# First layer's expert gate and up with the weights as stationary operand, half of the second layer's modulation on VectorE, final sums as columns

## The chip, the cores and the metric

The kernel runs on one core of one Trainium2 chip. The metric is the device time of one execution in microseconds; the median of three runs before the change is 1820.4 us (1817.2 to 1823.0).

## What is computed

Two layers over 512 latent and 256 context tokens of width 1024, all in fp32. Each layer mixes tokens (an mLSTM, a convolution and a Fourier group between one input and one output projection) and then routes tokens to 16 experts. The part that matters here, cut:

```python
def expert_choice_ffn(xn, w_router, w_gate, w_up, w_down):
    cap = EC_CAPACITY_FACTOR * n // N_EXPERTS
    aff = jax.nn.softmax(jnp.einsum('bnd,de->bne', xn, w_router).astype(jnp.float32), axis=-1)
    gate, idx = lax.top_k(jnp.swapaxes(aff, 1, 2), cap)
    xs = xn[bidx, idx]
    hid = jax.nn.silu(jnp.einsum('becd,edf->becf', xs, w_gate)) * jnp.einsum('becd,edf->becf', xs, w_up)
    ys = jnp.einsum('becf,efd->becd', hid, w_down) * gate[..., None].astype(xn.dtype)
    return jnp.zeros_like(xn).at[bidx, idx].add(ys)
...
    for l in range(DEPTH):
        mod = silu_c @ w_ada[l] + b_ada[l]
        sh1, sc1, gt1, sh2, sc2, gt2 = jnp.split(mod[:, None, :], N_ADA, axis=-1)
...
    return _rms(x, g_final).astype(x.dtype)
```

In the first layer latent and context tokens are both routed, each in its own set (64 and 32 tokens an expert); in the second only latent tokens are.

## The kernel before, in words

The program writes TensorE's order by hand; the order on the other engines is left to the framework's scheduler. Activations stand with features on the partitions. Each layer has three parts: the mixer (input projection `product`, L492, with a three-term split of the weights made by ScalarE L424 and VectorE L427), the output projection (eight blocks, the same `product`), and the expert stage. Small work that is not urgent hangs in `fills`: generators that `product` advances by a credit, so that their instructions land between its own.

One of these is `ada1`: the modulation vectors of the second layer, three rounds of `ada_round` (L284 to L297). A round streams 16 blocks of `w_ada` past two vectors on TensorE (L286, 32 x 256 in four column groups), copies the sums (L292) and turns them with four small products (L295). Its loads go over GpSimd's queue into a ring of 19 buffers. What is left of it is drained in the routing, before the gathered tokens are turned.

The expert stage works on pairs of experts, in the order gate of pair p+1, down of p, up of p+1. Weights come as 1 MB tiles (two blocks of 128 rows of an expert's matrix), eight tiles for a projection of a pair, loaded on SyncE's queue into `wreg` as buffers come free. `wide` runs one projection in four quarters. The tokens are the stationary operand, 32 of them in each column group of the array, and the weights run by in rows of 512: L1451 for the latent tokens (two experts x 64), L1461 for the context tokens (two experts x 32, in two halves). `gate` takes the Silu on ScalarE (L1487, L1489), `up` multiplies on VectorE (L1495, L1497). The hidden rows then have tokens on the partitions, so `up` queues transposes (L1503, 12 a pair) and copies (L1504) that `down` needs. Ahead of that the tokens of a pair are gathered by GpSimd (L1371), transposed on TensorE in `turn` (L1397, 8 for a latent pair, 8 for two context pairs) and modulated (L1402, L1404). `down` leaves its rows on the partitions of their tokens, and GpSimd adds them to a buffer in memory (L1555). In the second layer the tokens come from a one-hot product (L1394) and the last `down` is split in four with the final norm behind it: squares on ScalarE (L1693), summed by `rows` on TensorE (L1701), copied (L358) and turned into columns (L361).

Of the kernel before, what the change touches and what calls it, by code (L numbers as in the profile page):

```python
# [14 lines left out]
D = 1024  # L15
# [34 lines left out]
ADA1_RATE, AREG, ADA_XTK = 0.3, 19, 1.2  # L50
NACC = 6
VLAG = 0.0, 2.5
# [105 lines left out]
def build(nc, tc, xT, ctxT, params, w_ada, w_gates, w_in, w_out, w_router, w_e_gate, w_e_up, w_e_down,  # L158
          dft_l, dft_c, dft_ch, outT):
    RA_N, RB_N = 12288, 4608  # L160
    TOTAL = 53000 - RA_N - RB_N
# [3 lines left out]
    def body(A, RB, PS, scr, xrow, acc):  # L165
# [166 lines left out]
        def ada_scale(l, dst, m, gcol):  # L332
            for v in range(2):
                dve.scalar_tensor_tensor(dst[:, v], MOD[l][:, v, m * 8:(m + 1) * 8], 1.0, pc(l, gcol, 8),
                                         op0=OP.add, op1=OP.mult)
# [63 lines left out]
        for l in range(2):  # L399
# [712 lines left out]
            if not last:  # L1112
                areg = [mem.alloc(1024) for _ in range(AREG)]

                def ada1():
                    ring = Ring(areg)
                    for r in range(3):
                        yield from ada_round(1, r, ring, 5, pool, some=ADS[1])
                    ada_scale(1, A1[1], 1, P_G1)
                    ada_scale(1, A2[1], 4, P_G2)  # L1120
# [4 lines left out]
                fills.append(ada1f)  # L1125

# [12 lines left out]
            def load_experts(firsts=(), most=1000):  # L1139
                while len(wtiles) < min(wtaken[0] + len(wreg), len(wq), most):  # L1140
# [30 lines left out]
            for db in range(KB):  # L1171
# [22 lines left out]
                if db == 4:  # L1194
                    ride(0)
                for s in outs:
# [4 lines left out]
            ride(1)  # L1201
            fills.clear()
# [102 lines left out]
            if not last:  # L1305
                ada1f.drain()
                mem.free(areg)
# [30 lines left out]
            if not last:  # L1338
                slc_r, SLC = new(512)
                htc_r, hTc = new(4, 128)  # L1340
# [17 lines left out]
            XSp, XSq = {}, {}  # L1358
            if not last:
                xg_r = [mem.alloc(D) for _ in range(3)]  # L1360
                xs_r = [mem.alloc(KB * 128) for _ in range(2)]
                xgr = Ring(xg_r)
                xc_r = [mem.alloc(KB * 128) for _ in range(2)]
            fetched, gathers = {}, []

            def fetch_rows(s, i):

                t = fetched[s, i] = V((0, D, wp[4 + (s == CTX)][2]) if i == 0 else xgr.next(), D)
# [17 lines left out]
            def turn(s, i, hf):  # L1386
                def f():
                    dst = (XSp if s == LAT else XSq)[i]
                    b = bank67().rearrange("p (j t) -> p j t", j=4)
                    for j in range(4):  # L1390
                        db = 4 * hf + j
                        if last:
                            for c in range(4):
                                pe.matmul(b[:, j], XT[2 + c][:, db * 128:db * 128 + 128], onehots[i][:, c],  # L1394
                                          start=c == 0, stop=c == 3)
                        else:
                            pe.transpose(b[:, j], fetched[s, i][:, db * 128:db * 128 + 128], ident)  # L1397
# [473 lines left out]
```

## Time and profile before

| what | us |
|---|---|
| median of three runs | 1820.4 |
| the profiled execution | 1825.71 |
| its span | 1823.9 |
| TensorE busy | 1715.1 (94%) |
| weight loads of TensorE busy | 944.6 (52%) |
| VectorE busy | 628.5 (34%) |
| ScalarE busy | 447.5 (25%) |
| GpSimd busy | 150.7 (8%) |

Over the whole span TensorE is busy, but the page's slices show what stands behind that. In forty slices of 45.6 us, TensorE has nine tenths or more in nearly all; the DMA engines have nine tenths from slice 11 to 21 (the first layer's expert stage, about 400 GB/s) and again from slice 31 to 39 (the second layer's, 420 GB/s). The chain that ended last is followed back only to the second layer; in it DMA has 18% of the span and TensorE 14%. Matmuls are pipelined, so the time between the starts of equal instructions tells what one costs, and the idle time in brackets tells whether the engine waited.

### The profile page before, as it was taken

The page shows a single profiled execution, that of the slowest core. Times are in us where ns is not written, and L with a number is a line of the kernel's source. Part 1 is how long each engine was busy: PE and PEld are TensorE (multiplying, and loading weights), DVE is VectorE, ACT ScalarE, POOL GpSimd, SP SyncE. Part 2 cuts the span into 40 slices and gives each one's busy share as a digit, 9 for nine tenths or more (in the row PEclk, how much of TensorE's full clock was granted, in tenths as well). Part 3 has the DMA queues.
Part 4 walks back from the last instruction along what each step waited for, and adds up shares of the span by engine and source line. Part 5 has one row for each costly group of instructions (what it writes and reads, how often), then busy time and mean ns, then how long its engine had stood idle before and what let it go on. Part 6 is the DMA issues. An engine that isn't in the chain of part 4 may idle for free. (4 is left out here: it accounts for less than half of the span.)

```text
span 1823.9 us, 27692 instructions
## 1 busy us (share of the span) xinstructions
PE 1715.1 (94%) x11728; PEld 944.6 (52%) x11728; DVE 628.5 (34%) x1384; ACT 447.5 (25%) x861; POOL 150.7 (8%) x193
## 2 busy tenths in 40 slices
PE   6999999998999999999999999889979999999996
PEld 3678887876333333333233467777744444344433
DVE  4623897424101001001014677865230221112203
ACT  4433354413101101011000552356220101010002
POOL 1111121110101101100100001120000000000000
PEclk8999999998999999999999999999989999999999
DMA  9466344756999999999995113142669999999994
GB/s 384 150 209 195 106 128 157 243 209 233 386 420 402 402 421 403 402 418 404 399 393 213 35 47 97 60 130 96 244 251 421 421 421 420 420 421 421 420 421 193
DMA packets 94525, 529.59 MB, mean 290 GB/s; under 512 B 10177, under 2 KB 13249, under 8 KB 45505
## 3 DMA queue, kind: packets, MB, share of 16 engines
q1 hardware_dynamic: 75776, 459.66, 62.5%
q0 software_dynamic: 18624, 68.17, 11.6%
q8 instruction: 92, 1.51, 0.3%
q14 instruction: 33, 0.26, 0.0%
HBM read 513.10 MB, written 14.68 MB: 289 GB/s over the span
## 5 line engine op out<-in xcount | busy, mean ns | idle before, releaser
L492 PE MATMUL PS<-RA,RB 128*128 128x512 f32 (+1 forms) x2352 | 512.9, 365 | 18.8 <-DVE RB L427 6.0
L1451 PE MATMUL PS<-A 128*32 128x512 f32 (+1 forms) x2256 | 426.7, 595 | 5.8 <-DMA A<-w_e_up 5.2
L492 PEld LDWEIGHTS PS<-RA,RB 128*128 128x128 f32 x2352 | 375.7, 193 | 92.3 <-issue 18.1
L1451 PE MATMUL PS<-WP,A 128*32 128x512 f32 (+1 forms) x2160 | 370.1, 597 | 4.6 <-DMA WP<-w_e_up 4.6
L1451 PEld LDWEIGHTS PS<-A 128*32 128x32 f32 (+1 forms) x2256 | 128.4, 122 | 239.4 <-issue 220.9
L1451 PEld LDWEIGHTS PS<-WP,A 128*32 128x32 f32 (+1 forms) x2160 | 107.8, 117 | 199.0 <-issue 187.1
L1461 PE MATMUL PS<-WP,A 128*32 128x512 f32 x816 | 112.3, 594 | 0.0
L1021 DVE SCALAR_TENSOR_TENSOR A<-A 128x783 f32<-128x783 f32 (+1 forms) x120 | 107.5, 923 | 0.2
L1402 ACT ACTIVATE A<-PS,A 128x128 f32<-128x128 f32 x80 | 36.1, 458 | 245.2 <-DVE A L1404 244.6
L1461 PE MATMUL PS<-A 128*32 128x512 f32 x656 | 95.0, 606 | 0.0
L1504 ACT ACTIVATE A<-PS 128x512 f32<-128x512 f32 x40 | 22.3, 595 | 293.8 <-PE PS L1503 293.8
L424 ACT ACTIVATE RB<-A 128x1024 fp32r<-128x1024 f32 x60 | 63.4, 1059 | 123.7 <-PE PS L492 88.4
L1550 DVE TENSOR_SCALAR A<-PS,A 128x512 f32<-128x512 f32 x6 | 4.5, 751 | 243.9 <-PE PS L1451 243.9
L1517 DVE SCALAR_TENSOR_TENSOR A<-PS,A 128x512 f32<-128x512 f32 x80 | 56.5, 746 | 88.2 <-PE PS L1516 87.5
L1524 DVE SCALAR_TENSOR_TENSOR RB<-PS,A,RB 128x512 fp32r<-128x512 f32 x18 | 13.5, 751 | 205.8 <-ACT RB L1523 205.0
L1404 DVE TENSOR_SCALAR A<-PS,A 128x128 f32<-128x128 f32 x80 | 32.7, 409 | 141.2 <-PE PS L1397 86.0
L427 DVE TENSOR_TENSOR RB<-A,RB 128x1024 fp32r<-128x1024 f32 x50 | 63.0, 1265 | 17.2 <-ACT RB L424 14.7
L1394 PEld LDWEIGHTS PS<-A 128*128 128x128 f32 x512 | 59.3, 196 | 7.2 <-DVE A L1495 4.9
L284 POOL DMA_DIRECT2D A<-w_ada x80 | 42.5, 535 | 235.7 <-PE PS L286 136.3
L1394 PE MATMUL PS<-A 128*128 128x128 f32 x512 | 61.0, 281 | 0.4 <-DVE A L1381 0.4
L1495 DVE TENSOR_TENSOR A<-PS,A 128x512 f32<-128x512 f32 x32 | 22.1, 692 | 109.3 <-PE PS L1451 109.3
L1461 PEld LDWEIGHTS PS<-WP,A 128*32 128x32 f32 x816 | 27.9, 110 | 54.6 <-issue 54.6
(332 smaller groups left out, 1600.9 us busy)
## 6 DMA issues: line engine op xcount, KB each, us to landing
A<-w_e_gate SPq DMA_DIRECT2D x75, 1024.0 KB, 15.7
A<-w_e_up SPq DMA_DIRECT2D x66, 1024.0 KB, 15.3
WP<-w_e_down SPq DMA_DIRECT2D x63, 1024.0 KB, 17.3
A<-w_e_down SPq DMA_DIRECT2D x63, 1024.0 KB, 17.3
WP<-w_e_up SPq DMA_DIRECT2D x62, 1024.0 KB, 14.4
WP<-w_e_gate SPq DMA_DIRECT2D x53, 1024.0 KB, 17.1
A<-w_ada POOLq DMA_DIRECT2D x80, 512.0 KB, 4.7
A<-w_in SPq DMA_DIRECT2D x44, 512.0 KB, 3.6
```

Source lines behind the costliest of these rows:

```text
L284: after(eng.dma_start(w, src[r, hf, k]), firsts if hf == 0 and k < len(ring.regs) else ())
L424: whi.append(act.activation(h, raw[i], AF.Copy))
L427: wlo.append(eng.tensor_tensor(lo, raw[i], h.bitcast(F32), OP.subtract))
L492: pe.matmul(banks[s][:, :LEN[s]], w[:, k], xin[:, j, k, OFF[s]:OFF[s] + LEN[s]], start=k == k0 and i == 0, stop=k == k1 and i == 2)
L1021: dve.scalar_tensor_tensor(o, i, wcol, o, op0=OP.mult, op1=OP.add)
L1394: pe.matmul(b[:, j], XT[2 + c][:, db * 128:db * 128 + 128], onehots[i][:, c], start=c == 0, stop=c == 3)
L1402: act.activation(dst[:, db], b[:, j], AF.Identity, bias=sh_, scale=sc_)
L1404: dve.tensor_scalar(dst[:, db], b[:, j], sc_, sh_, op0=OP.mult, op1=OP.add)
L1451: pe.matmul(B(o + hf)[c:c + wd, :], lhs(k, e)[:, c % 64:c % 64 + wd], w[e][:, a, hf * 512:hf * 512 + 512], start=k == 0, stop=k == KB - 1, ...
L1461: pe.matmul(B(o + 2)[32 * g:32 * g + 32, :], lhsc(k, e), w[e][:, a, hf * 512:hf * 512 + 512], start=k == 0, stop=k == KB - 1, tile_positio ...
L1504: act.activation(dst, b, AF.Copy)
L1517: dve.scalar_tensor_tensor(X[LAT][:, db], b, MOD[l][:, LAT, 40 + db:41 + db], X[LAT][:, db], op0=OP.mult, op1=OP.add)
```

## The change

In the first layer `tall` takes the place of `wide` for gate and up. A weight tile is now laid out as all eight blocks of rows by 256 columns of an expert (`layout`), so that two tiles, one of each expert, make a quarter. A 128 x 128 block of weights is the stationary operand, and the 96 tokens of the expert (64 latent, 32 context, side by side in `XSp`) run by. The result has features on the partitions, as `down` wants it: transposes and copies of hidden rows go, and Silu and product are done a quarter at a time. The context half of `turn` becomes a product of the gathered rows with 64 columns of the identity, for one pair at a time. `down` of the first layer stays as it was.

Of the second layer's modulation only round 0 stays on TensorE. Rounds 1 and 2 are multiplied and added on VectorE (`ada1_rest`, 32 passes over 1024 elements, for the latent vector alone), and `ada1_sums` adds over the partitions with products by ones and turns the sums. Both run as fills of the output projection and end before the routing. The ring has 15 buffers, six for round 0 and nine for the rest.

In the second layer there is one more weight buffer, and the final sums of squares come as columns at once (`cols`). The scratch for GpSimd's descriptors is halved to make room.

```diff
-ADA1_RATE, AREG, ADA_XTK = 0.3, 19, 1.2
+ADA1_RATE, AREG, ADA_XTK = 0.3, 15, 1.2
 NACC = 6
+ADA1V_RATE = 0.55
...
-    TOTAL = 53000 - RA_N - RB_N
+    TOTAL = 55040 - RA_N - RB_N
...
                 def ada1():
-                    ring = Ring(areg)
-                    for r in range(3):
-                        yield from ada_round(1, r, ring, 5, pool, some=ADS[1])
+                    yield from ada_round(1, 0, Ring(areg[:6]), 5, pool, some=ADS[1])
                     ada_scale(1, A1[1], 1, P_G1)
-                    ada_scale(1, A2[1], 4, P_G2)
+                acc_r, ACC = new(2, 2, 1024)
+                def ada1_rest():
+                    ring = Ring(areg[6:])
+                    for r in (1, 2):
+                        for hf in range(2):
+                            for k in range(KB):
+                                w = V(ring.next(), 1024)
+                                pool.dma_start(w, w_ada[1, r, hf, k])
+                                a = ACC[:, r - 1, hf]
+                                if k == 0:
+                                    dve.tensor_scalar(a, w, cs[:, k, 0:1], None, op0=OP.mult)
+                                else:
+                                    dve.scalar_tensor_tensor(a, w, cs[:, k, 0:1], a, op0=OP.mult, op1=OP.add)
+                                yield 1.0
+                def ada1_sums():
+                    rows_r, rows = new(2, 512)
+                    for r in range(2):
+                        for hf in range(2):
+                            for g in range(4):
+                                pe.matmul(B(6 + r)[32 * g:32 * g + 32, hf * 256:hf * 256 + 256], ones[:, 0:32],
+                                          ACC[:, r, hf, g * 256:g * 256 + 256], start=True, stop=True,
+                                          tile_position=(0, 32 * g))
+                        act.activation(rows[:, r], B(6 + r), AF.Copy)
+                    yield 3.5
+                    for r in range(2):
+                        p2 = B(6 + r)[:, 0:32].rearrange("p (b v g) -> p b v g", b=4, v=2)
+                        for b in range(4):
+                            pe.matmul(p2[:, b], rows[:, r, b * 128:(b + 1) * 128], selg[:, 0], start=True, stop=True)
+                        m = 16 + r * 16
+                        dve.tensor_tensor(MOD[1][:, 0, m:m + 16].rearrange("p (g b) -> p g b", g=4),
+                                          p2[:, :, 0, :].rearrange("p b g -> p g b"),
+                                          bada(1, m, m + 16).rearrange("p (g b) -> p g b", g=4), OP.add)
+                    ada_scale(1, A2[1], 4, P_G2, (0,))
+                    mem.free(rows_r)
...
+                ada1v = Fill(ada1_rest(), ADA1V_RATE)
+                fills.append(ada1v)
...
-                        t = V(wreg[len(wtiles) % len(wreg)], 2, D)
-                        r = sp.dma_start(t, w[l, e, i].rearrange("p (a f) -> p a f", a=2))
+                        a = 2 if last or w is w_e_down else KB
+                        t = V(wreg[len(wtiles) % len(wreg)], a, 2 * D // a)
+                        r = sp.dma_start(t, w[l, e, i].rearrange("p (a f) -> p a f", a=a))
...
+                if db == KB - 2 and not last:
+                    ada1v.drain()
+                    fills.append(Fill(ada1_sums(), 0.6))
...
-                extra = mem.alloc(2048, top=True)
-            sl_r, SLT = new(1024)
-            ht_r, hT = new(KB, 128)
+                extra = [mem.alloc(2048, top=True) for _ in range(2)]
+            sl_r, SLT = new(1024) if last else new(KB, 2, CL + CC)
+            ht_r, hT = new(KB, 128) if last else new(KB, 2, CL + CC)
...
+                            c0 = i % 2 * 64
+                            pe.matmul(b[:, j], fetched[s, i // 2][:, db * 128:db * 128 + 128], ident[:, c0:c0 + 64],
+                                      start=True, stop=True)
...
+                            o = dst[:, db, :, 0:CL] if s == LAT else dst[:, db, :, CL:CL + CC]
+                            v = b[:, j].rearrange("p (e t) -> p e t", e=2)
...
+            def tall(p, fill, out):
+                banks = [next_set() + i for _ in range(2) for i in range(2)]
+                for q in range(4):
+                    w = wtiles[wtaken[0]:wtaken[0] + 2]
+                    wtaken[0] += 2
+                    b = B(banks[q])[:, 0:4 * (CL + CC)].rearrange("p (f e t) -> p f e t", f=2, e=2)
+                    for e in range(2):
+                        for fb in range(2):
+                            for k in range(KB):
+                                pe.matmul(b[:, fb, e], w[e][:, k, fb * 128:fb * 128 + 128], XSp[p][:, k, e],
+                                          start=k == 0, stop=k == KB - 1)
+                    out(2 * q, b)
+                    fill(q)
+                    load_experts()
...
             def gate(p, fill):
+                if not last:
+                    tall(p, fill, lambda k, b: act.activation(SLT[:, k:k + 2], b, AF.Silu))
+                    return
                 o = wide(*tokens(p), fill)
                 pop(trans, 99)
                 for hf in range(2):
                     act.activation(SLT[:, hf * 512:hf * 512 + 512], B(o + hf), AF.Silu)
+            def up(p, fill):
                 if not last:
-                    act.activation(SLC, B(o + 2), AF.Silu)
-            def up(p, fill):
+                    tall(p, fill, lambda k, b: dve.tensor_tensor(hT[:, k:k + 2], b, SLT[:, k:k + 2], OP.mult))
+                    return
                 o = wide(*tokens(p), fill)
                 for hf in range(2):
                     t = SLT[:, hf * 512:hf * 512 + 512]
                     dve.tensor_tensor(t, B(o + hf), t, OP.mult)
-                if not last:
-                    dve.tensor_tensor(SLC, B(o + 2), SLC, OP.mult)
                 def tr_(src, dst, eng):
                     def f():
                 for hf in range(2):
                     trans.append(tr_(SLT[:, hf * 512:hf * 512 + 512], hT[:, 4 * hf:4 * hf + 4], act))
-                if not last:
-                    trans.append(tr_(SLC, hTc, dve))
...
-                def rows(dbs):
+                def cols(dbs):
                     for db in dbs:
-                        g = db % 4
-                        pe.matmul(fin[32 * g:32 * g + 32], ones[:, 0:32], sqs[db], start=db < 4, stop=db > 3,
-                                  tile_position=(0, 32 * g))
+                        for c in range(4):
+                            pe.matmul(fin[:, 4 * db + c:4 * db + c + 1], sqs[db][:, c * 128:c * 128 + 128], ones[:, 0:1],
+                                      start=True, stop=True)
...
+                        if qd == 3 and k == 3:
+                            cols((2, 3))
+                            pop(scat, 99)
...
-                    if qd == 3:
-                        rows(range(4))
+                    if qd == 2:
+                        cols((0, 1))
...
-                rows((4, 5))
+                cols((4, 5))
                 pop(scat, 99)
-                rows((6, 7))
-                fsum[0] = Sums(LAT, fin)
+                cols((6, 7))
+                fsum[0] = fin[:, 0:4 * KB]
...
-        rs = row_rstd(fsum[0], B(6), V(tring.next(), TL), sm, act)
+        dve.tensor_reduce(sm, fsum[0].rearrange("p (k c) -> p c k", c=4), AX.X, OP.add)
+        rstd_small(sm, sm, 1.0 / D)
+        rs = B(6)
+        spread(sm, 4, V(tring.next(), TL), rs)
...
+        if n != "w_e_down":
+            a[n][0] = f(n)[0].reshape(E, KB, 128, 4, 256).transpose(0, 3, 2, 1, 4).reshape(E, 4, 128, 2 * D)
...
-    nc = bacc.Bacc("TRN2", target_bir_lowering=False, num_devices=1)
+    nc = bacc.Bacc("TRN2", target_bir_lowering=False, num_devices=1, dynamic_dma_scratch_size=8192)
```

Before, TensorE in the first layer's expert stage: the last quarter of the first gate and the first quarter of the first up, with the tokens as stationary operand (L1397 turns the next tokens).

```order
L1451 MATMUL PS<-A 32x512 x16
L1461 MATMUL PS<-A 32x512 x8
L1451 MATMUL PS<-A 32x512 x16
L1397 MATMUL PS<-A 128x128 x8
L1461 MATMUL PS<-A 32x512 x8
```

After, the same place and the quarter behind it (L1509 is `tall`, L1449 and L1446 the context and latent turns).

```order
L1509 MATMUL PS<-A 128x96 x64
L1449 MATMUL PS<-A 128x64 x8
L1446 MATMUL PS<-A 128x128 x4
L1509 MATMUL PS<-A 128x96 x16
L1509 MATMUL PS<-A,WP_3269 128x96 x16
```

A quarter has gone from 24 products of 512 columns to 32 of 96 columns, and the turns stand between quarters instead of inside one.

Before, TensorE from the last block of the output projection to the first turns (L1230 to L1303 routing, L286 and L295 `ada_round`).

```order
L1230 MATMUL PS<-A,WP_3258 128x17 x6
L1257 MATMUL PS<-A,WP_3258 96x128 x2
L1281 MATMUL PS<-A 128x128 x48
L295 MATMUL PS<-A 128x8 x4
L286 MATMUL PS<-A 32x256 x8
L1303 MATMUL PS<-A,WP_3259 128x96 x2
L286 MATMUL PS<-A 32x256 x56
L295 MATMUL PS<-A 128x8 x4
L1397 MATMUL PS<-A,WP_3259 128x128 x8
```

After, the same place (L1279 to L1352 routing).

```order
L1279 MATMUL PS<-A,WP_3273 128x17 x6
L1306 MATMUL PS<-A,WP_3273 96x128 x2
L1330 MATMUL PS<-A 128x128 x48
L1352 MATMUL PS<-A,WP_3274 128x96 x2
L1449 MATMUL PS<-A 128x64 x8
L1446 MATMUL PS<-A,WP_3273 128x128 x8
```

The index transposes now follow the token transposes at once, and the turns follow them.

After, VectorE in the middle of the output projection (L1133 and L1135 `ada1_rest`, L428 the weight split, L1229 the residual sum).

```order
L428 TENSOR_TENSOR RB<-A,RB 128x1024
L1135 SCALAR_TENSOR_TENSOR A<-A 128x1024 x6
L1133 TENSOR_SCALAR A<-A 128x1024
L1229 SCALAR_TENSOR_TENSOR A<-PS,A 128x512
L1229 SCALAR_TENSOR_TENSOR A<-PS,A 128x256
L428 TENSOR_TENSOR RB<-A,RB 128x1024
L1135 SCALAR_TENSOR_TENSOR A<-A 128x1024 x5
```

The new passes stand between a block's weight split and its residual sum.

## Rows read from the trace of the kernel before

**Rows 1.** Busy time by stretch, in the first layer's expert stage.

```profile
core 0: us, PE busy (x) PEld busy (x) DVE busy (x) ACT busy (x) POOL busy (x), PEclk, DMA share, GB/s
530.00:590.00 60.00, 60.00 (x556) 19.43 (x552) 6.11 (x12) 7.83 (x15) 7.71 (x6) 1.00 1.02 406
```

**Rows 2.** Timeline of TensorE in that stage: start, length, line, tile, shape, count.

```profile
585.66 1.09 PE L1503 MATMUL PS<-A 128*128 128x128 f32 x8
...
594.30 3.62 PE L1451 MATMUL PS<-WP,A 128*32 128x512 f32 x32
597.74 1.90 PE L1461 MATMUL PS<-WP,A 128*32 128x512 f32 x16
599.45 3.62 PE L1451 MATMUL PS<-WP,A 128*32 128x512 f32 x32
...
650.51 1.09 PE L1503 MATMUL PS<-A 128*128 128x128 f32 x8
```

**Rows 3.** Groups by shape, weight loads: busy us, mean ns of one | idle before.

```profile
L1461 PEld LDWEIGHTS PS<-WP,A 128*32 128x32 f32 x816 | 27.9, 110 | 54.6 <-issue 54.6
...
L1183 PEld LDWEIGHTS PS<-A 128*128 128x128 f32 x48 | 5.6, 190 | 0.1
```

**Rows 4.** Timeline of TensorE: loads of 128 columns with 1, 16, 128 moving columns.

```profile
1261.68 1.84 PE L957 MATMUL PS<-A 128*128 128x1 f32 x16
...
1280.76 1.85 PE L1183 MATMUL PS<-A 128*128 128x16 f32 x16
...
1350.65 3.84 PE L1394 MATMUL PS<-A 128*128 128x128 f32 x32
```

**Rows 5.** One line's instructions: ns shortest/median/longest, first and last start.

```profile
L1183 PE MATMUL PS<-A x48: 177/263/263, 354.0 to 1282.4; 128*128 128x16 f32 x48
...
L1394 PE MATMUL PS<-A x512: 274/275/582, 1341.3 to 1727.4; 128*128 128x128 f32 x171
```

**Rows 6.** Busy time by stretch, columns as in rows 1, other stretches.

```profile
340.00:432.00 92.00, 91.98 (x710) 66.46 (x708) 18.13 (x29) 15.53 (x25) 15.65 (x31) 0.98 0.61 211
358.00:361.00 3.00, 3.00 (x12) 2.07 (x15) 0.98 (x1) 0.00 (x0) 0.00 (x0) 0.50 0.28 66
1341.00:1360.00 19.00, 18.22 (x106) 11.74 (x108) 2.64 (x8) 1.83 (x4) 0.00 (x0) 0.91 0.33 119
1640.00:1648.00 8.00, 5.37 (x26) 1.67 (x24) 1.50 (x2) 1.26 (x2) 0.00 (x0) 1.00 1.01 419
```

**Rows 7.** Timeline of TensorE and ScalarE, first layer's output projection and routing.

```profile
353.97 3.64 PE L1183 MATMUL PS<-A 128*128 128x16 f32 x32
...
401.91 1.07 PE L286 MATMUL PS<-A 128*32 128x256 f32 x16
402.92 1.43 PE L492 MATMUL PS<-RA,RB 128*128 128x256 f32 x8
...
448.90 0.31 ACT L1300 ACTIVATE WP<-WP 32x128 f32<-32x128 f32 x1
...
450.08 1.94 PE L286 MATMUL PS<-A 128*32 128x256 f32 x16 [0.42 <-DVE A L297]
451.95 0.58 PE L1303 MATMUL PS<-A,WP 96*128 96x96 f32 x2
452.46 8.12 PE L286 MATMUL PS<-A 128*32 128x256 f32 x112
```

**Rows 8.** Groups by shape, VectorE's weight split.

```profile
L427 DVE TENSOR_TENSOR RB<-A,RB 128x1024 fp32r<-128x1024 f32 x50 | 63.0, 1265 | 17.2 <-ACT RB L424 14.7 <-PE PS L826 2.0
```

**Rows 9.** Chain that ended last, second layer: start, length, what.

```profile
1746.53 19.85 DMA A<-w_e_up
...
1802.05 0.99 PE PS L1701 x8
...
1809.08 1.72 PE PS L1701 x4
...
1810.82 0.61 ACT A L358
...
1811.47 1.07 PE PS L361 x8
```

More of the change, by code (lines that the diff above doesn't have):

```diff
@@ L330, in ada_first, with ada_scale @@
                 yield
-        def ada_scale(l, dst, m, gcol):
-            for v in range(2):
+        def ada_scale(l, dst, m, gcol, vs=(0, 1)):
+            for v in vs:
                 dve.scalar_tensor_tensor(dst[:, v], MOD[l][:, v, m * 8:(m + 1) * 8], 1.0, pc(l, gcol, 8),
@@ L1201, in body @@
             ride(1)
+            if not last:
+                fills[-1].drain()
+                mem.free([areg[6:], acc_r])
             fills.clear()
@@ L1306, in body @@
                 ada1f.drain()
-                mem.free(areg)
+                mem.free(areg[:6])
             GXu = GX.bitcast(mybir.dt.uint32)
@@ L1357, in body @@
                 oh_r = [mem.alloc(512)]
-            XSp, XSq = {}, {}
+            XSp = {}
             if not last:
                 xg_r = [mem.alloc(D) for _ in range(3)]
-                xs_r = [mem.alloc(KB * 128) for _ in range(2)]
+                xs_r = [mem.alloc(KB * 2 * (CL + CC)) for _ in range(2)]
                 xgr = Ring(xg_r)
-                xc_r = [mem.alloc(KB * 128) for _ in range(2)]
+                ac_r = mem.alloc(D)
             fetched, gathers = {}, []
             def fetch_rows(s, i):
-                t = fetched[s, i] = V((0, D, wp[4 + (s == CTX)][2]) if i == 0 else xgr.next(), D)
+                t = fetched[s, i] = V((0, D, wp[4][2]) if s == LAT and i == 0 else xgr.next(), D)
                 col = i if s == LAT else NP + i
@@ L1387, in f @@
                 def f():
[L1388 to L1391, printed above, removed]
+                    dst = XSp[i]
+                    b = bank67().rearrange("p (j t) -> p j t", j=4 if s == LAT else KB)
+                    dbs = range(4 * hf, 4 * hf + 4) if s == LAT else range(KB)
+                    for j, db in enumerate(dbs):
                         if last:
@@ L1413, in fetch_pair @@
                     fetch_rows(CTX, q // 2)
-                    XSq[q // 2] = V(xc_r[q // 2 % 2], KB, 128)
-                    turns.extend(turn(CTX, q // 2, hf) for hf in range(2))
                 if last:
                     turns.append(onehot(q))
+                    XSp[q] = V(xs_r[q % 2], KB, 128)
                 else:
                     fetch_rows(LAT, q)
-                XSp[q] = V(xs_r[q % 2], KB, 128)
+                    XSp[q] = V(xs_r[q % 2], KB, 2, CL + CC)
+                    turns.append(turn(CTX, q, 0))
                 turns.extend(turn(LAT, q, hf) for hf in range(2))
@@ L1435, in body, with next_set @@
             wd = 64 if last else 32
+            def next_set():
+                sets[0] += 1
+                return (sets[0] - 1) % 2 * 3
+            def tall(p, fill, out):
[12 more added lines that the diff above has]
+                    load_experts()
             def wide(lhs, lhsc, fill):
-                o = sets[0] % 2 * 3
-                sets[0] += 1
+                o = next_set()
                 for q in range(4):
@@ L1479, in tokens @@
             def tokens(p):
-                return (lambda k, e: XSp[p][:, k, 64 * e:64 * e + 64],
-                        lambda k, e: XSq[p // 2][:, k, p % 2 * 64 + 32 * e:p % 2 * 64 + 32 * e + 32])
+                return lambda k, e: XSp[p][:, k, 64 * e:64 * e + 64], None
             def gate(p, fill):
+                if not last:
+                    tall(p, fill, lambda k, b: act.activation(SLT[:, k:k + 2], b, AF.Silu))
+                    return
                 o = wide(*tokens(p), fill)
@@ L1561, in collect @@
                 AL = [V(r, 4, 512) for r in al_r]
-                AC = [V(xgr.next(), D) for _ in range(2)]
+                AC = [V(r, D) for r in (xg_r[0], ac_r)]
                 for hf in range(2):
```

30 lines of the change are left out of this document (16 added, 14 removed).

## The prediction

> **What bounds the kernel now.** I read the busy time by stretch first. In the first layer's expert stage TensorE is busy 60.00 us of a 60 us stretch at a granted clock of 1.00, that is the 2.4 GHz level, while VectorE has 6.11 us and ScalarE 7.83 us of work [rows 1]. The DMA engines show full too, at 406 GB/s, but TensorE never stops for a weight there, so a TensorE instruction added or taken away in this stage moves the end by its own length. The timeline of one expert pair then gives the prices. One quarter of a projection (32 latent and 16 context instructions) runs from 594.30 to 599.45, 5.15 us, so a projection of an expert pair takes 4 x 5.15 = 20.6 us. The first transposes of two neighbouring pairs start at 585.66 and 650.51: a pair takes 64.85 us [rows 2]. Three projections are 61.8 us of that; the remaining 3.0 us are 24 transposes (12 of the hidden rows, 8 of latent tokens, 4 of context tokens on average), 0.126 us each. The second layer's expert stage waits on its weights instead, and the first layer's mixer and output projection are TensorE work again (91.98 of 92 us busy between 340 and 432 us) [rows 6].
>
> **Part 1: gate and up (the term that decides).** A projection today is 96 fp32 products, two instructions each, 192 in all, each streaming 512 columns, four side by side in column groups: 20.6 us / 192 = 107 ns an instruction. The new form has 128 products (2 experts x 4 quarters x 2 blocks x 8 contraction blocks) for the pair, 256 instructions, each with a full 128 x 128 block of weights to load and 96 columns to stream. The streaming sum is the same (192 x 512 columns by four groups side by side, or 256 x 96 alone: 24576 both times), so the question is the load. A load takes 110 ns with 32 columns and 190 ns with 128 [rows 3]: 80 ns for 96 columns, so I estimate 107 ns of loading for 128 columns over a fixed part, against 96/512 of the 427 ns that 512 columns take (four side by side, 107 each), 80 ns, of streaming. What loads cost back to back stands in [rows 4]: sixteen instructions with 128-column weights and only 16 moving columns take 1.85 us; less the 0.263 us of the last one [rows 5], 15 steps of 106 ns. Sixteen with one single moving column: (1.84 - 0.26) / 15 = 105 ns. Thirty-two with 128 moving columns: (3.84 - 0.275) / 31 = 115 ns. So the step does not shrink below 106 ns however few columns run by, and at 128 columns it is 115, not the 214 of load plus stream: the two overlap, and the longer sets the step. A 96-column instruction lies between, 106 to 115 ns. I take 107, since 80 ns of streaming leaves the load in the lead as in the 16-column row. One projection then takes 256 x 0.107 = 27.4 us (27.1 to 29.4), 6.78 us more than now, and there are 16 of them: +108.5 us (+104 to +141). Nothing covers this, since TensorE is the engine without a gap.
>
> The Trainium skill, "TensorE: Matmul & The Clock Gate", section "Part 3: Packing small matmuls — row/col tiling", says that a weight load overlaps a running matmul only when the two use different row groups. All instructions here use all rows, so by that rule the step would be load plus stream, 187 ns as an estimate, and the sum would be a rival below. The 128-column row disagrees: 115 ns [rows 4].
>
> **Part 2: transposes and token turns.** The 96 transposes of the hidden rows disappear: 96 x 0.126 = -12.1 us. The latent turns stay. The context turns were 32 transposes, 4.0 us; now each pair makes 8 true fp32 products of 64 columns, 16 instructions, 128 in all, at the 106 ns of a loaded block: 13.6 us. Net +9.6 us. Results now go out by quarter: ScalarE's four Silu passes and VectorE's four products of 384 columns a projection lie under 6.8 us quarters on engines that are nearly idle [rows 1]; the bank that a quarter writes was read at least two quarters before. Weights are asked for more slowly than now, so I see no DMA wait. Expert stage in sum: 108.5 - 12.1 + 9.6 = +106.0 us.
>
> **Part 3: the second layer's modulation vectors.** Round 1 leaves TensorE's stream in the output projection: eight groups of 16 instructions, 1.01 us each (401.91 to 402.92) [rows 7], -8.1 us. Round 2 sat in the routing chain, where ScalarE has the last routing value ready at 449.21, but the transposes of indices start at 451.95, behind the group at 450.08 [rows 7]: -2.7 us, since gathers and first turn follow from there. The rest of round 2, from 452.46, covers the gathers; I count no gain for it (at most 3 us more). Added on TensorE are 32 instructions of 256 columns at the price of two such groups, 2.0 us, and 16 loads of 128 columns, 1.7 us: +3.7 us. On VectorE come 32 passes over 1024 elements; the nearest row is the weight split of the same width, 1265 ns [rows 8], so about 40 us. VectorE has only 18.1 us of work between 340 and 432 us [rows 6], but it works in order, and each pass waits for a load issued by GpSimd. Queued behind such a pass are the weight splits and the residual sums that TensorE's next block needs. I take +2.5 us of stall, with 0 and +10 as bounds. Sum -4.6 us, from -10 to +3. The smaller scratch for GpSimd's descriptors has no row; all GpSimd transfers here are hidden or small, so it stays inside this bound.
>
> **Part 4: second layer.** One more 1 MB buffer: the DMA engines are busy only 0.33 of 1341 to 1360 us, for lack of a free buffer; a weight lands every 19.85 / 8 = 2.5 us later on, where the DMA sets the pace [rows 6, 9]. One tile more ahead of that is -2.5 us (0 if the tile only waits elsewhere). The final sums of squares as columns: today 0.99 us of products, twice 1.72, then a 0.61 us copy and 1.07 us of columns [rows 9]. Now 64 loads of 128 columns, 6.8 us, of which the last 8 follow the last square. The end loses 0.61 + 1.07 us and about 0.8 us of product; some 2.4 us of extra load sits ahead of it, half of it in waits. Sum -1 us (-3 to +2).
>
> **Sum.** 106.0 - 4.6 - 2.5 - 1.0 = +97.9 us. The profiled execution took 1825.7 us, so it would become about 1923.6; it lies 5.3 us above the median of 1820.4, and against the median I forecast 1918. Low ends together: 104 - 2.5 - 10 - 2.5 - 3 = +86, 1906. High ends: 141 - 2.5 + 3 + 0 + 2 = +143, 1964.
>
> **The rivals.** (a) The load hides and streaming sets the step: 81 ns, 20.7 us a projection, +2 - 2.5 - 8.1 = -8.6 us, 1812, faster. For it speaks that streaming work is equal before and after; against it, that the 16-column row keeps 106 ns with hardly any streaming [rows 4]. It decides below a step of 83 ns, where the saved transposes pay. Chance 0.05, of which 0.01 is no change. (b) Load and stream add up, 187 ns: 47.9 us a projection, 16 x 27.3 = +437, 2247. Against it the 115 ns. Chance 0.02. (c) TensorE falls to its 1.2 GHz level: a step would double to 214 ns, a projection to 54.8 us, and the whole to about 2357. For it speaks a row: behind 32 instructions of the 16-column kind at 353.97 [rows 7] the granted clock was 0.50 from 358 to 361 us although TensorE had not waited [rows 6]. Against it: from 1640 to 1648 us TensorE waited for weights, was busy 5.37 of 8 us, and kept 1.00 [rows 6]. No row has products of the new kind for as long. Chance 0.05. That nothing moves is excluded: the instruction order shows 128 products of 96 columns.
>
> **How the numbers follow.** The forecast has 0.88. Its error comes from the step above all: each ns of it is 16 x 256 x 0.001 = 4.1 us. I cut the joint ends a little: 1900 to 1955 should hold 0.8. Slower by over 0.3% (about what a measurement of this kernel can tell from no change): 0.95; faster 0.04; within it 0.01.
>
> **What would show it.** In the profile after, the new products' line should step by 107 ns with loads of 190 ns and no gap, a quarter should take 6.8 us instead of 5.15, a pair 78 us, and the DMA rate in that stage should fall from 406 to about 340 GB/s. Right on vectors: output projection shorter by 5 us, index transposes 2.7 us earlier behind the routing. A step of 81 ns makes the forecast wrong on its sign, one of 115 makes it too low.

## The result

The changed kernel takes 1930.6 us (median of 4 runs, 1928.5 to 1932.4) against 1820.6 us for the kernel before on the same chip: a ratio of 1.060, 95% interval 1.058 to 1.062. That is 110 us slower, where +98 was forecast; 1930.6 lies inside the forecast's range. The profiled execution has a span of 1930.4 us, 106.5 more than before; before's profiled execution (1825.71 us) lay 5.3 us above its median, after's 1.8, which is the difference between 106.5 and 110.

### The profile page after: what moved, and what is told of

Same layout as the page of the kernel before. It is cut to its first block, busy times and chain, and to the rows that moved or that the text cites. A ratio compares the mean times of both kernels' runs of the same rounds, so it can differ in the third digit from the quotient of the medians.

```text
span 1930.4 us, 29477 instructions
## 1 busy us (share of the span) xinstructions
PE 1822.1 (94%) x12568; PEld 1305.5 (68%) x12568; DVE 668.9 (35%) x1438; ACT 439.0 (23%) x860; POOL 150.2 (8%) x193
## 3 DMA queue, kind: packets, MB, share of 16 engines
q0 software_dynamic: 18624, 68.17, 10.7%
## 5 line engine op out<-in xcount | busy, mean ns | idle before, releaser
L1528 PE MATMUL PS<-A 128*64 128x512 f32 (+1 forms) x1384 | 293.7, 594 | 4.3 <-DMA A<-w_e_up 3.8
L1509 PE MATMUL PS<-A,WP 128*128 128x96 f32 x2336 | 267.0, 276 | 0.0
L1509 PEld LDWEIGHTS PS<-A,WP 128*128 128x128 f32 x2336 | 265.2, 193 | 2.6 <-issue 2.5
L1528 PE MATMUL PS<-WP,A 128*64 128x512 f32 (+1 forms) x984 | 201.5, 594 | 4.0 <-DMA WP<-w_e_up 4.0
L1528 PEld LDWEIGHTS PS<-A 128*64 128x64 f32 (+1 forms) x1384 | 91.7, 128 | 167.8 <-issue 151.1
L1509 PEld LDWEIGHTS PS<-A 128*128 128x128 f32 x1760 | 198.3, 192 | 2.6 <-issue 2.5
L1509 PE MATMUL PS<-A 128*128 128x96 f32 x1760 | 200.0, 275 | 0.0
L1528 PEld LDWEIGHTS PS<-WP,A 128*64 128x64 f32 (+1 forms) x984 | 59.9, 124 | 109.0 <-issue 98.5
L1459 ACT ACTIVATE A<-PS,A 128x64 f32<-128x64 f32 (+1 forms) x96 | 40.6, 439 | 352.7 <-DVE A L1461 351.9
L428 DVE TENSOR_TENSOR RB<-A,RB 128x1024 fp32r<-128x1024 f32 x50 | 63.2, 1269 | 15.3 <-ACT RB L425 12.8
L1443 PEld LDWEIGHTS PS<-A 128*128 128x128 f32 x512 | 60.1, 198 | 7.2 <-DVE A L1575 4.9
L1461 DVE TENSOR_SCALAR A<-PS,A 128x64 f32<-128x64 f32 (+1 forms) x96 | 36.2, 387 | 79.5 <-PE PS L1443 48.5
```

What stands on the lines that cost most here:

```text
L428: wlo.append(eng.tensor_tensor(lo, raw[i], h.bitcast(F32), OP.subtract))
L1459: act.activation(o, v, AF.Identity, bias=sh_, scale=sc_)
L1461: dve.tensor_scalar(o, v, sc_, sh_, op0=OP.mult, op1=OP.add)
L1509: pe.matmul(b[:, fb, e], w[e][:, k, fb * 128:fb * 128 + 128], XSp[p][:, k, e], start=k == 0, stop=k == KB - 1)
L1528: pe.matmul(B(o + hf)[c:c + wd, :], lhs(k, e)[:, c % 64:c % 64 + wd], w[e][:, a, hf * 512:hf * 512 + 512], start=k == 0, stop=k == KB - 1, ...
```

## The profile after

**The expert stage.** First the busy time of the same stretch as in [rows 1] (start and end, then per engine the busy us and the number of instructions, the granted clock, DMA share, GB/s).

```profile
530.00:590.00 60.00, 60.00 (x545) 45.31 (x544) 3.38 (x8) 5.66 (x12) 5.71 (x4) 1.00 0.91 330
```

TensorE still has no gap and the granted clock is still 1.00, the 2.4 GHz level; the DMA rate is down from 406 to 330 GB/s, since the weights are asked for more slowly. The timeline of TensorE over one pair answers to [rows 2] (start, length, line, tile, shape, count; L1509 is `tall`, L1449 the context turn, L1446 the latent turn, L1528 and L1538 `down`).

```profile
573.83 3.81 PE L1509 MATMUL PS<-A 128*128 128x96 f32 x32
...
581.05 1.92 PE L1449 MATMUL PS<-A 128*128 128x64 f32 x16
582.81 0.61 PE L1446 MATMUL PS<-A 128*128 128x128 f32 x4
583.26 14.43 PE L1509 MATMUL PS<-A,WP 128*128 128x96 f32 x128
...
601.51 18.03 PE L1509 MATMUL PS<-A 128*128 128x96 f32 x160
619.37 14.46 PE L1509 MATMUL PS<-A,WP 128*128 128x96 f32 x128
633.76 3.64 PE L1528 MATMUL PS<-WP,A 128*32 128x512 f32 x32
...
654.50 5.71 PE L1509 MATMUL PS<-A,WP 128*128 128x96 f32 x49
```

The 160 instructions from 601.51 to 619.37 take 17.86 us, 111.6 ns each, and the 128 behind them 112. A projection is therefore 256 x 0.1116 = 28.6 us instead of 20.6, and a pair runs from 573.83 to 654.50, 80.7 us instead of 64.85. The groups by shape show the lengths of single instructions (busy us, mean ns of one, idle before).

```profile
L1509 PE MATMUL PS<-A,WP 128*128 128x96 f32 x2336 | 267.0, 276 | 0.0
L1509 PEld LDWEIGHTS PS<-A,WP 128*128 128x128 f32 x2336 | 265.2, 193 | 2.6 <-issue 2.5
```

A load lasts 193 ns and a product 276, yet they step by 112: a load and a product of neighbouring instructions are under way at the same time, and neither number is the price of one.

**Output projection and routing**, TensorE's timeline (in brackets idle time and what ended it), answering to [rows 7].

```profile
328.36 0.67 PE L379 MATMUL PS<-A 128*128 128x256 f32 x2 [2.51 <-DVE A L378]
...
348.61 1.68 PE L493 MATMUL PS<-RA,RB 128*128 128x256 f32 x9 [0.64 <-DVE A L1229]
...
431.30 1.82 PE L1279 MATMUL PS<-A,WP 128*128 128x17 f32 x12
...
448.02 0.58 PE L1352 MATMUL PS<-A,WP 96*128 96x96 f32 x2 [3.47 <-ACT WP L1349]
454.53 3.67 PE L1449 MATMUL PS<-A 128*128 128x64 f32 x16 [5.93 <-DMA A<-xrow,A]
...
461.54 1.12 PE L1446 MATMUL PS<-A,WP 128*128 128x128 f32 x4 [2.48 <-ACT A L1459]
462.44 12.76 PE L1509 MATMUL PS<-A,WP 128*128 128x96 f32 x93
```

The same timeline in the kernel before (L1230 and L1279 open the routing, L1397 are the turns, L1451 the first expert product):

```profile
432.05 1.82 PE L1230 MATMUL PS<-A,WP 128*128 128x17 f32 x12
...
462.24 1.07 PE L1397 MATMUL PS<-A,WP 128*128 128x128 f32 x8
...
466.70 5.52 PE L1451 MATMUL PS<-WP,A 128*32 128x512 f32 x32
```

The projection ends only 0.75 us earlier than before (431.30 against 432.05) although a round of modulation has left it, because TensorE now waits for VectorE. The index transposes come 3.9 us earlier (448.02 against 451.95), but then the gather of tokens is late: 5.93 us of waiting, and from 454 to 462 us, where the turns behind it run, the granted clock is 0.50.

**A stall that is gone.** Late in the stage TensorE reads back the latent rows that GpSimd has added up in memory and transposes them (L1572 before, L1649 after). In the kernel before this cost more than the transposes. Its timeline and its busy time by stretch:

```profile
911.49 1.09 PE L1572 MATMUL PS<-A 128*128 128x128 f32 x4 [4.35 <-DMA A<-accl]
912.51 3.64 PE L1461 MATMUL PS<-A 128*32 128x512 f32 x16
915.92 4.49 PE L1451 MATMUL PS<-A 128*32 128x512 f32 x32
```

```profile
905.00:910.00 5.00, 2.14 (x20) 0.39 (x12) 0.00 (x0) 0.00 (x0) 0.00 (x0) 1.00 1.02 410
910.00:915.00 5.00, 3.51 (x16) 1.32 (x20) 0.75 (x1) 0.00 (x0) 0.00 (x0) 0.59 1.01 406
```

TensorE waits 4.35 us for the read, which stands in full DMA queues (share 1.02); the granted clock then drops to 0.59, and the next two groups take 3.41 and 4.42 us from start to start instead of 1.72 and 3.55 elsewhere, 2.6 us more: 6.9 us together. In the changed kernel's timeline the same read is there in time.

```profile
1015.56 0.60 PE L1649 MATMUL PS<-A 128*128 128x128 f32 x4
```

## Experiments: what sets the step

The kernels of this section were each run once; the argument rests on the steps in their traces, not on small differences of their times.

Each product was cut into two of 48 columns (twice the loads, the same columns in all):

```diff
-    pe.matmul(b[:, fb, e], w[e][:, k, fb * 128:fb * 128 + 128], XSp[p][:, k, e], ...)
+    for t0 in (0, 48):
+        kk, h0 = (2 * k + t0 // 48) % KB, (2 * k + t0 // 48) // KB * 48
+        pe.matmul(b[:, fb, e, h0:h0 + 48], w[e][:, kk, fb * 128:fb * 128 + 128], XSp[p][:, kk, e, h0:h0 + 48], ...)
```

> The changed kernel with every product of gate and up cut in two of 48 columns: twice the loads of 128 columns, the same columns streamed. Theory A (the load sets the step): 512 instructions of about 108 ns a projection, 55 us instead of 28.5, 16 times, so about 2355 us. Theory B (streaming plus a fixed part of some 30 ns sets the step of 111 ns): 70 ns a step, 36 us a projection, about 2050 us. Theory C (streaming alone): about 1930 us.

It took 3220.9 us, more than any theory said. The stretch of [rows 1] in its trace:

```profile
530.00:590.00 60.00, 60.00 (x283) 60.00 (x282) 0.00 (x0) 0.98 (x2) 0.00 (x0) 0.50 0.25 88
```

The granted clock is 0.50, the 1.2 GHz level, with TensorE busy for all 60 us. The 60 us hold 283 products, 212 ns each. Behind a `down` of 512-column products the clock is 1.00 for a few us, and there the same products show what they cost at the upper level. Timeline and busy time:

```profile
1541.76 4.41 PE L1512 MATMUL PS<-A,WP 128*128 128x48 f32 x38
```

```profile
1541.50:1546.00 4.50, 4.50 (x41) 4.50 (x42) 0.00 (x0) 0.69 (x1) 2.62 (x2) 1.00 1.04 383
```

Less the 0.275 us that one of them lasts there, 4.41 us are 37 steps of 111.8 ns, what 96 columns take. So 48 columns are no cheaper than 96 per instruction: twice the steps are 4096 x 0.1116 = 457 us of the 1290 us by which this kernel is behind the changed one, and the rest goes with the clock.

Half of each load, with the columns as they were (64 of each block's 128 features are left out, so half of the hidden rows stay zero):

```diff
-    pe.matmul(b[:, fb, e], w[e][:, k, fb * 128:fb * 128 + 128], XSp[p][:, k, e], ...)
+    pe.matmul(b[0:64, fb, e], w[e][:, k, fb * 128:fb * 128 + 64], XSp[p][:, k, e], ..., tile_position=(0, 0))
```

> The changed kernel with only the first 64 of each block's 128 features computed in gate and up (the other hidden features are left at zero): loads of 64 columns, the same number of instructions, the same 96 columns streamed. Theory A (the load sets the step): with 53 ns of load the 80 ns of streaming lead, a step of 82 to 90 ns, 16 x 256 x 0.025 = 100 us less, about 1830 us. Theory B (a fixed price of an instruction of some 105 ns, whatever it loads): about 1930 us, unchanged.

1820.6 us. TensorE's timeline:

```profile
572.45 13.36 PE L1510 MATMUL PS<-A 128*64 128x96 f32 x160
585.65 10.72 PE L1510 MATMUL PS<-A,WP 128*64 128x96 f32 x128
```

13.20 us for 160 is 82.5 ns a step: with the load halved the step falls to what 96 columns cost (the 80 ns of the prediction), and the 110 us are back. A fixed price per instruction is out.

Both halves, in two column groups, so that the whole product is computed with twice the instructions:

```diff
+    for c in (0, 64):
+        pe.matmul(b[c:c + 64, fb, e], w[e][:, k, fb * 128 + c:fb * 128 + c + 64], XSp[p][:, k, e], ..., tile_position=(0, c))
```

> The changed kernel with each block of weights split into two blocks of 64 columns that stand in two column groups of the array: twice the instructions, half the load each, 96 columns through each group. Theory A with loads of two groups side by side: the pair steps by 82 to 90 ns, so about 1830 us. Theory A with loads one after the other: 107 to 112 ns a pair, about 1920 us. Theory B (a fixed price of an instruction of some 105 ns): 210 ns a pair, about 2340 us.

1841.6 us, 89 less than the changed kernel with the same work. Timeline:

```profile
566.14 10.78 PE L1510 MATMUL PS<-A,WP 128*64 128x96 f32 x256
576.86 0.66 PE L1446 MATMUL PS<-A 128*128 128x128 f32 x4
...
588.00 5.50 PE L1510 MATMUL PS<-A 128*64 128x96 f32 x127 [0.54 <-issue]
```

From 566.14 to the next start at 576.86 a pair of instructions takes 84 ns, against 82.5 for one half alone, so the two groups' loads and streams run side by side. All 128 features are computed here, so it is not their number that makes 111.6 ns but the load of 128 columns as one. There are gaps of up to 1.1 us put down to "issue" (TensorE is busy 58.70 of 60 us from 530 to 590); what is late there, at 42 ns an instruction, the profile does not show. They sum to 15.4 us, enough for the 12 us between 1841.6 and the forecast 1830.

Then the columns alone, 64 and 128 instead of 96 with full loads:

```diff
-    pe.matmul(b[:, fb, e], w[e][...], XSp[p][:, k, e], ...)
+    pe.matmul(b[:, fb, e, 0:64], w[e][...], XSp[p][:, k, e, 0:64], ...)                                  # x9
+    pe.matmul(b[:, fb, e], w[e][...], XSp[p][:, k].rearrange("p e t -> p (e t)")[:, 64 * e:64 * e + 128], ...)   # x10
```

> The changed kernel with only the 64 latent tokens as moving columns of gate and up; the context tokens' gate and up are left out, their hidden rows are zero. 4096 instructions as before, 64 columns each instead of 96. Theory F (the step grows evenly with the columns between the two rows of the trace of before, 106 ns at 16 and 115 ns at 128): (64 - 16) / 112 x 9 = 3.9, a step of 110 ns, 4096 x (110 - 111.5) = -6 us, 1924. Theory G (the load alone sets the step as long as the columns take less time than it, as the prediction took it; the 4.5 ns above 107 at 96 columns come from elsewhere): 64 columns change nothing, 111.5 ns, 1930. Theory H (a plain 107 up to some number of columns, and a rise behind it): 107 ns, 1912. If the granted clock falls as with 48 columns: about 214 ns, 2350 or more.

> The changed kernel with 128 moving columns in gate and up instead of 96: the 96 tokens of the expert and 32 of the other expert of the pair, whose results are not used. 4096 instructions as before. Theory F: a step of 115 ns as in the row of before, 4096 x (115 - 111.5) = +14 us, 1945. Theory G: the load alone sets it, 111.5 ns, 1930.

With 128 columns the kernel took 1934.0 us. TensorE's timeline:

```profile
600.61 18.03 PE L1510 MATMUL PS<-A 128*128 128x128 f32 x160
618.48 14.46 PE L1510 MATMUL PS<-A,WP 128*128 128x128 f32 x128
```

17.87 us for 160, 111.7 ns, against 111.6 with 96 columns. With 64 columns the kernel took 2014.9 us, and its timeline and clock say why:

```profile
564.04 20.58 PE L1510 MATMUL PS<-A,WP 128*128 128x64 f32 x96
...
681.74 18.03 PE L1510 MATMUL PS<-A 128*128 128x64 f32 x160
```

```profile
560.00:600.00 40.00, 40.00 (x190) 40.00 (x190) 1.80 (x6) 1.37 (x4) 0.94 (x1) 0.50 0.45 156
...
640.00:650.00 10.00, 10.00 (x100) 2.76 (x92) 0.00 (x0) 0.00 (x0) 0.00 (x0) 1.00 0.97 392
...
700.00:800.00 100.00, 100.00 (x906) 81.59 (x909) 5.59 (x17) 7.61 (x24) 8.55 (x7) 1.00 0.90 330
```

From the first product at 463.56 to the first `down` at 632.34 the clock stays at 0.50 and a step takes 212 ns (20.37 us for 96). The changed kernel takes 90.65 us for the same stretch (462.44 to 553.09) and this one 168.78, so 78 of the 84 us between the two kernels are lost there. Behind the 512-column products of `down` the clock is 1.00 again and stays there, and the same 64-column products step by 111.6 ns (17.86 for 160). So theory G holds: at the upper level 48, 64, 96 and 128 columns step alike, within 0.2 ns; F and H fall. The 128-column load sets it.

## Experiments: the rest of the change

**Everything but `tall`**: vectors, buffers and final sums as changed, gate and up as before:

```diff
-    tall(p, fill, lambda k, b: act.activation(SLT[:, k:k + 2], b, AF.Silu))
+    o = wide(*tokens(p), fill)
```

> The kernel before, with all of the change except the new gate and up: modulation rounds 1 and 2 on VectorE, the extra weight buffer and the sums as columns stay. Theory A (gate and up carry the whole loss; the other parts gain what the two traces show up to the first expert product, 466.70 to 462.44, and behind it, 1.6 us for the buffer, 0.7 us lost at the end): 5 us below the kernel before, 1815 us. The wait of 4.35 us for the memory sums (at 907 us before) should still be there. Theory B (part of the loss sits in the vectors on VectorE or in the halved descriptor scratch, through late gathers): at or above 1821 us.

1818.4 us against 1822.2 for the kernel before on that chip, a ratio of 0.9975 (0.9960 to 0.9989): about 4 us faster. So the whole loss belongs to `tall` with the turns that it needs, as forecast. The read-back of the sums still waits in its timeline, and pays the low clock:

```profile
906.29 1.09 PE L1620 MATMUL PS<-A 128*128 128x128 f32 x4 [3.89 <-DMA A<-accl]
907.31 3.64 PE L1509 MATMUL PS<-A 128*32 128x512 f32 x16
```

**The read-back later.** On that kernel, TensorE's read-back in the gate of the last pair starts two quarters later:

```diff
-    (lambda q: (pop(scat), pop(trans, (0, 2, 1, 0)[q])))
+    (lambda q: ((q > 1 or p < NACC) and pop(scat), pop(trans, (0, 2, 1, 0)[q])))
```

> The kernel of x1_wide_rest with one order changed: TensorE reads the latent tokens back from memory, for the residual sum, two quarters later in the last pairs' gate. Theory D (about 7 us of the new kernel's loss were covered because it lost a wait for that read-back, 4.35 us in the kernel before at 911.49 and 3.89 us in x1, and the low clock behind it): the wait goes and so does the fall of the clock, 5 to 7 us, 1812 to 1814 against 1818.4 for x1. Rival E (DMA engines are full there, so what is not waited for at that read is waited for at the next weight or the next read): 1818, the wait only moves.

1812.8 us, a ratio of 0.9950 (0.9933 to 0.9967) to before. Timeline and clock at the same place:

```profile
907.09 1.09 PE L1551 MATMUL PS<-A 128*128 128x128 f32 x8
...
913.40 0.66 PE L1620 MATMUL PS<-A 128*128 128x128 f32 x4
```

```profile
910.00:915.00 5.00, 5.00 (x52) 1.92 (x44) 0.75 (x1) 0.41 (x1) 0.00 (x0) 1.00 1.01 410
```

No wait and no fall of the clock, though the DMA engines are as full as before. The first product of the stage's last `down` starts at 976.81 instead of 984.19, 7.4 us earlier; 1.2 of that were there at the first expert product (461.37 against 462.55), ahead of the edit, so the stage is 6.2 us shorter. The medians are 5.5 us apart, taken on two chips on which the kernel before differs by 1.6. Theory D holds, and the version beats both kernels, by 7.8 and 118 us.

**Rounds 1 and 2 back on TensorE**, in the changed kernel:

```diff
+    ring = Ring(areg)
+    for r in range(3):
+        yield from ada_round(1, r, ring, 5, pool, some=ADS[1])
```

> The changed kernel with rounds 1 and 2 of the second layer's modulation back on TensorE. By the prediction's part 3 they are worth 4.6 us: 1930.6 + 4.6 = 1935. By the trace of after, where the output projection gained 0.75 us and the first expert product starts 4.3 us earlier: +4.3, 1935 as well. Rival (VectorE's stalls eat the gain, and the gather waits eat the rest): no change, 1930.6.

1941.3 us, +10.7, more than either theory. Timeline:

```profile
353.94 4.10 PE L1184 MATMUL PS<-A 128*128 128x16 f32 x32
...
367.53 1.07 PE L286 MATMUL PS<-A 128*32 128x256 f32 x16
...
469.38 5.79 PE L1461 MATMUL PS<-A,WP 128*128 128x96 f32 x36
```

The first expert product starts at 469.38 instead of 462.44, +6.9. Some 1.6 us of that are clock: behind the 16-column products that start at 353.94 the second group of L286 comes at 367.53, while in the kernel before, with the same work and a start at 353.97 [rows 7], it comes at 365.91; the granted clock from 358 to 364 is 0.52 here and 0.72 there. Another 1.5 us are lost in the tail, where the last 16 column sums take 3.50 us instead of 1.95 at a lower clock. What is left, 5 us at the first expert product and 8 by the medians, is the worth of the two rounds; how often the two falls of the clock come is open.

**Final sums as rows again:**

```diff
-    pe.matmul(fin[:, 4 * db + c:4 * db + c + 1], sqs[db][:, c * 128:c * 128 + 128], ones[:, 0:1], ...)
+    pe.matmul(fin[32 * g:32 * g + 32], ones[:, 0:32], sqs[db], ..., tile_position=(0, 32 * g))
```

> The changed kernel with the final sums of squares as rows, as before the change. Prediction: the columns save 1 us, so this gives 1931.6. By the trace of after, where the tail is 0.65 us longer than before: 1930, 0.6 us faster. Under 0.3% either way; the tail in the trace decides it.

1928.5 us, 2 less. The tail doesn't show it: from the first product of the last `down` to the end it takes 41.6 us (1885.43 to 1927.0), and 41.3 in the changed kernel (1889.12 to 1930.4), 40.7 before (1783.23 to 1823.9). The 3.4 us by which this execution is ahead stand in parts that are the same code (the second layer's first turns start 2.5 us earlier). Columns or rows is worth nothing that can be seen here.

**One extra buffer instead of two:**

```diff
-    extra = [mem.alloc(2048, top=True) for _ in range(2)]
+    extra = [mem.alloc(2048, top=True) for _ in range(1)]
```

> The changed kernel with one extra weight buffer in the second layer instead of two. Prediction: one tile ahead is worth 2.5 us, so 1933. By the trace of after, where the wait for the last weight ends 1.6 us earlier relative to the routing than before: 1932.2. Rival: the buffer only waits elsewhere, 1930.6.

1933.0 us, +2.5. From the second layer's first turns to the last `down` it takes 442.2 us (1447.75 to 1889.92) against 440.4 (1448.72 to 1889.12): 1.8 us for one tile, near the forecast's 2.5.

## Why the prediction was right, and where its sizes were off

**The step of gate and up (mis-sized).** Mechanism and sign were right: a 128-column load sets the step, products of 96 columns don't hide it, and nothing covers TensorE. The size was 111.6 ns, not 107: 16 x (28.57 - 20.6) = +127.5 us against +108.5, which is the largest error of the sum. The prediction took the 16-column row (106 ns) as the bare load and the 128-column row (115 ns) as load plus some streaming [rows 4]. The runs with 48, 64 and 128 columns show that streaming plays no part there, so the two rows were not ends of one line. In the changed kernel the 16 context turns of 64 columns step by 110 ns (581.05 to 582.81), and its final sums hold a row with one moving column (TensorE's timeline):

```profile
1907.08 1.95 PE L1779 MATMUL PS<-A 128*128 128x1 f32 x16
```

The last one lasts 0.25 us, so a step is 1.70 / 15 = 113 ns, at a granted clock of 1.00 and a DMA share of 0.00 (1907.1 to 1908.8), where [rows 4] gave 105 for the same shape. So neither the columns nor the DMA engines account for the 105 to 115 ns of a 128-column load; what does stays open.

The Trainium skill, "TensorE: Matmul & The Clock Gate", section "LDWEIGHTS (loading the stationary operand)", gives a load of P columns P / 1.2 ns, 107 for 128. The step of 111.6 lies 4% above it, and the 82.5 of the halved load is not half, since the 80 ns of streaming are longer there. Its rule on overlap, which the prediction set against the 115 ns row, would have given an estimated 187 ns, and no step here shows that at the upper clock.

**Hidden-row transposes, turns.** Forecast -12.1, measured -15.0 (one pair, times eight). They stood inside `wide`, and an interruption costs more than its instructions: with the gap on either side eight cost 1.16 us and four 0.72, which makes 1.88 us a pair. The context turns in the stage cost 7 x 1.76 = 12.3 us instead of 3 x 1.16 = 3.5, +8.8 (forecast +9.6 for all of them); the latent turns, now between quarters, cost 0.44 for four, about 1.9 us less in all. 127.5 - 15.0 + 8.8 - 1.9 = +119.4.

**The stall (missing from the prediction).** From the first expert product to the first product of the stage's last `down` the trace shows +111.6 us (462.44 to 1096.76 against 466.70 to 989.46), not 119.4. The last `down` in TensorE's timeline, before and after:

```profile
989.46 1.07 PE L1639 MATMUL PS<-A 128*32 128x512 f32 x8
```

```profile
1096.76 1.06 PE L1716 MATMUL PS<-A 128*32 128x512 f32 x8
```

The 6.9 us of the read-back's wait and of the low clock behind it are most of the difference. The prediction wrote "TensorE never stops for a weight there" from [rows 1]; that is true of the weights and of that stretch, but it had not looked at the end of the stage, where TensorE stops for something else. This error and the step's partly cancel: with the step right and the rest as forecast, the sum would have been +117.

**Vectors.** Forecast -4.6 in all. At the first expert product the trace shows -4.3, the kernel without `tall` about 4 us at its end, the reverse edit 5 to 8 without the clock. The sum is right, its parts are not. The output projection gained 0.75 us instead of 8.1 - 3.7 - 2.5 = 1.9 (from 300 to 432 us TensorE's waits sum to 3.6 us, against 0.4 before); the 5 us among the prediction's signs do not follow from these terms. The index transposes came 3.9 us earlier, 3.2 of them gained in the routing against a forecast of 2.7. The rest of round 2, for which the prediction counted no gain, was worth 3.8 us: its last products no longer stand ahead of the first turn, which starts 7.7 us earlier (454.53 against 462.24). The turns gave 3.4 of that back: up to the first expert product they take 7.9 us instead of 4.5, with a longer wait, more instructions and a granted clock of 0.50. Two terms that the prediction lacked cancel here, so that the sum came out near is in part luck. The largest wait, 2.51 us at 328.36, is for VectorE's L378, which stands behind the new passes in VectorE's timeline; other passes wait for their loads:

```profile
326.54 1.28 DVE L1135 SCALAR_TENSOR_TENSOR A<-A 128x1024 f32<-128x1024 f32 x1
327.74 0.47 DVE L378 TENSOR_SCALAR A<-A 128x128 f32<-128x128 f32 x2
...
345.02 1.28 DVE L1135 SCALAR_TENSOR_TENSOR A<-A 128x1024 f32<-128x1024 f32 x1 [1.36 <-DMA A<-w_ada]
...
346.88 1.28 DVE L1135 SCALAR_TENSOR_TENSOR A<-A 128x1024 f32<-128x1024 f32 x1
348.07 0.48 DVE L1229 SCALAR_TENSOR_TENSOR A<-PS,A 128x256 f32<-128x256 f32 x1
```

The residual sum L1229 at 348.07 stands right behind such a pass as well. It is what TensorE waited for at 348.61.

**Second layer.** The extra buffer: -1.6 us in the trace of after and 1.8 in the reverse edit, forecast -2.5. The final columns: about +0.6 us in the tail against -1, none in the reverse edit.

**The rivals.** (a), that the load hides, fell: it needed 83 ns, and only half a load gives that. (b) fell with the step. (c), the 1.2 GHz level, did not happen in the stage but was nearer than its 0.05: with 48 columns it holds through most of the stage and comes back behind a `down` without a gap in TensorE's work (1.00 until 1546 us, 0.50 from 1547), with 64 it holds until the first `down`. The changed kernel's stage begins at 0.50 too, and its clock is back within 8 us:

```profile
462.00:466.00 4.00, 4.00 (x21) 4.00 (x20) 0.82 (x2) 0.92 (x2) 0.00 (x0) 0.50 0.66 225
466.00:470.00 4.00, 4.00 (x33) 4.00 (x32) 0.00 (x0) 0.00 (x0) 0.00 (x0) 0.86 1.00 420
```

The row from 1640 to 1648 us that spoke against (c) was of the second layer's 512-column products; the other row, behind the 16-column products [rows 6], deserved more than 0.05.

## What to carry to other kernels

Weights as the stationary operand want columns that run by for at least as long as the load takes: here one 128-column load per 96 columns made 111.6 ns of what had been 80 ns of streaming, and turned results were worth only 15 us against 127. Where the stationary side must be wide, half-width loads in two column groups run side by side: 84 ns a pair in the one run that shows it. Before a term is added up from a stage's mean, read that stage's longest waits to its end: a 4 us wait with the low clock behind it was worth 5 to 6 us to remove, at least as much as the rest of the change.

## What the runs showed of the hardware

- In the kernel with 64 columns the granted clock stayed at 0.50 for 169 us (463 to 632) though TensorE had no gap. It was 1.00 behind a `down` of 512-column products, and the same 64-column products then ran at 1.00 to the end of the stage. With 96 and with 128 columns it rose from 0.50 within the first 8 us. The Trainium skill, "TensorE: Matmul & The Clock Gate", section "What's actually happening", says that activity releases the throttle; the 64-column kernel shows an engine busy for 169 us that is not released.
- In the kernel with 48 columns the granted clock went from 1.00 (1541.5 to 1546 us) to 0.50 (1547 to 1564) while TensorE worked without a gap.
- Behind the router's 16-column products (from 353.97 us before the change, 358.17 after it, 353.94 in the kernel with the rounds back on TensorE) the granted clock fell while TensorE was busy throughout: it was 0.72 from 358 to 364 us before, 0.77 from 362 to 368 after, and 0.52 from 358 to 364 in the third.
- A step at the lower level took 212 ns with 48 and with 64 columns, which would be 106 at the upper one, while 111.8 and 111.6 were measured there. The difference has no explanation here.
